# A float32 layer from split products: two more classical chunks, another order of the first product, and a shorter way into the MLP

## The chip, the cores and the metric

The kernel runs on one core of a Trainium2 chip. The metric is the device time of one execution in microseconds (us): the median of several runs. The trace of one profiled execution gives start and length of every instruction on the engines: TensorE (PE, with its weight loads as PEld), VectorE (DVE), ScalarE (ACT), GpSimd (POOL) and SyncE (SP, which issues the DMAs).

## The reference

One layer on 256 tokens of width 1024, all in float32: a mixer with four head groups, and behind it the channel sub-layer on which the change works.

```python
for l in range(DEPTH):                       # DEPTH = 1
    h = rms_norm(x, pre_mix_g[l])
    u = h @ w_in[l]                          # 1024 x 2560
    ...                                      # conformer conv, short conv, attention, RG-LRU
    y = jnp.concatenate([y_a, y_b, y_c, y_d], axis=-1) @ w_out[l]
    x = x + rms_norm(y, post_mix_g[l])
    h = rms_norm(x, pre_mlp_g[l])
    m = jnp.square(jax.nn.relu(h @ mlp_w1[l])) @ mlp_w2[l]   # 1024 x 4096, 4096 x 1024
    x = x + rms_norm(m, post_mlp_g[l])
return x
```

## The kernel before, in words

**Split products.** Every float32 operand is split into a rounded part `hi` and the rest `lo` (ACT copies to `hi`, DVE subtracts to `lo`), and a product is three matmuls: hi·hi, hi·lo and lo·hi. In the trace `hi_w`, `lo_w` are such parts of an MLP weight, `h2T`, `h2L` those of the normalised activations h, and `mh`, `ml` those of m = relu(h W1)².

**Chunks.** The hidden width 4096 is cut into 16 chunks of 256. For chunk c, `up(c)` multiplies h with its columns of W1 into one PSUM bank `pm` (two halves j, eight blocks k, three matmuls each: 48 matmuls of 256 columns). `relu2` reads the bank on ACT (tile `mr`, then the square, tile `mf`). A product with the chunk's rows of W2 follows, accumulated in PSUM banks over the chunks.

**Two forms of the second product.** The product of m and W2 of one chunk is a 2 by 2 by 2 product of blocks. Chunks in `SEVEN` (1 to 12) use a form with seven block products (Strassen's idea, Winograd's sums): `t_sums` forms sums of weight blocks on DVE (tile `trs`), `t_hi`/`t_lo` split them (`th` on ACT, `tl` on DVE), `act_sums` forms sums of m, and `down7` issues 7 x 3 = 21 matmuls of 512 columns. Chunk 0 uses the classical `EIGHT`: 24 matmuls, no sums of weights, and one sum of m. Chunks 13 to 15 go into the final pieces, `last_down(n, t, h)` (chunk n, token tile t, piece h).

**Order.** The instructions of every engine stand in the order in which the program is written. An iteration c of the main loop splits the weights W1 of c+1 and W2 of c, forms and splits the sums, takes relu² of chunk c, issues `down7(c-1)`, and then `up(c+1)`. So PE runs up(c+1), down7(c), up(c+2), down7(c+1) and so on. `up(c+1)` reuses the one bank `pm`, and starts when ACT's `mr` has read chunk c from it. W1 and W2 come as tiles of 1 MiB by DMA into four buffers `raw`.

**Chunk 0** differs: its first product (`pz`, by `up0`) has tokens on the partitions, so `act0`, called between the halves of `up(1)`, transposes m on PE (bank `ptm`), copies it back to `mf`, and forms the sum and the two parts.

**Squares of x.** The last norm needs a factor per token, `q2`, from the sum of squares of `x1`. It is computed ahead of chunk 1: two ACT instructions (tile `scr`) and four short ones on DVE.

Of the kernel before, what the change touches and what calls it, by code (L numbers as in the profile page):

```python
# [16 lines left out]
F32 = mybir.dt.float32  # L17
F32R = mybir.dt.float32r
BF16 = mybir.dt.bfloat16
AF = mybir.ActivationFunctionType  # L20
ALU = mybir.AluOpType
# [3 lines left out]
P = 128  # L25
S = 256
D = 1024
KT = D // P
NW = 2048
# [36 lines left out]
def hybrid_layer(ctx, tc, x, head, win, wout, w1, w2, gates, rows, out):  # L66
    nc = tc.nc
    V, A, G, T, Q = (InOrder(tc, e) for e in (nc.vector, nc.scalar, nc.gpsimd, nc.tensor, nc.sync))

    cst = ctx.enter_context(tc.tile_pool(name="cst", bufs=1))  # L70
    wts = ctx.enter_context(tc.tile_pool(name="wts", bufs=4))
# [3 lines left out]
    wk = wk_ctx.__enter__()  # L75
# [3 lines left out]
    def pbank(tag, name):  # L79
        return pacc.tile([P, 512], F32, tag=tag, name=name)  # L80
# [5 lines left out]
    def sm(name):  # L86
        return in_turn("sm", name)
# [12 lines left out]
    raw, hi, lo = {}, {}, {}  # L100

    def new_raw(n):
        k = seq[n]
        raw[k] = wts.tile([P, NW], F32, tag="raw", name=f"raw_{k[0]}{k[1]}")
        return raw[k], src[k[0]][k[1]]

    def load(n, parts=1):
        if n < len(seq):
            w, d = new_raw(n)
            for i in range(parts):  # L110
                c = slice(i * NW // parts, (i + 1) * NW // parts)
                Q.dma_start(w[:, c], d[:, c])

    def part(i, parts):
        return slice(i * NW // parts, (i + 1) * NW // parts)
# [26 lines left out]
    c = 0  # L142
    for blocks in HEAD:
        n = HOFF[blocks[-1]] + S
        Q.dma_start(hd[:, c:n], head[:, c:n])
        c = n
# [570 lines left out]
    h2 = big.tile([P, KT, S], F32R, tag="hT", name="h2T")  # L717
    h2L = big.tile([P, KT, S], F32R, tag="hL", name="h2L")
# [124 lines left out]
    wk = ctx.enter_context(tc.tile_pool(name="wk2", bufs=2))  # L843
# [13 lines left out]


    FORMS = 13
    SEVEN = range(1, FORMS)  # L860
    BLOCK = {(0, 0): 0, (1, 1): 1, (1, 0): 2, (0, 1): 3}
    B = 512
    mf, mh, ml, th, tl = {}, {}, {}, {}, {}

    def up(c, between=None):
        pu = pbank("mm0", f"pm{c}")
        H, L = hi["w1", c], lo["w1", c]
        for j in range(2):
            if j and between:
                between()  # L870
            o = pu[:, j * S:(j + 1) * S]
            for k in range(KT):
                ws = slice(k * S + j * P, k * S + (j + 1) * P)
                T.matmul(o, H[:, ws], h2[:, k, :], start=(k == 0), stop=False)
                T.matmul(o, H[:, ws], h2L[:, k, :], start=False, stop=False)
                T.matmul(o, L[:, ws], h2[:, k, :], start=False, stop=(k == KT - 1))
        return pu

    def relu2(c, pu):
        r = wk.tile([P, 512], F32, name="mr", bufs=1)  # L880
        A.activation(r, pu, AF.Relu)
        m = mf[c] = wk.tile([P, 8 * P], F32, name="mf", bufs=2)
        A.activation(m[:, :512], r, AF.Square)

    def mblocks(c, i, n=1):
        return mf[c][:, i * P:(i + n) * P]

    def act_sums(c):

        if c not in SEVEN and c < FORMS:  # L890
            pairs = mf[c][:, :4 * P].rearrange("p (i t n) -> p i t n", t=2, n=P)
            V.tensor_tensor(mblocks(c, 4, 2).rearrange("p (i n) -> p i n", n=P), pairs[:, :, 1], pairs[:, :, 0],
                            op=ALU.subtract)
        elif c < FORMS:
            V.tensor_tensor(mblocks(c, 4), mblocks(c, 0), mblocks(c, 1), op=ALU.subtract)
            V.tensor_tensor(mblocks(c, 5, 2).rearrange("p (i n) -> p i n", n=P),
                            mf[c].rearrange("p (i n) -> p i n", n=P)[:, 0:5:4, :],
                            mblocks(c, 2)[:, None, :].to_broadcast([P, 2, P]), op=ALU.add)
            V.tensor_tensor(mblocks(c, 7), mblocks(c, 3), mblocks(c, 6), op=ALU.subtract)

    def act_cols(c):
        return slice(P, 8 * P) if c in SEVEN else slice(0, (6 if c < FORMS else 4) * P)

    def act_hi(c):
        cs = act_cols(c)
        mh[c] = wk.tile([P, 8 * P], F32R, name="mh", bufs=2)
        A.activation(mh[c][:, cs], mf[c][:, cs], AF.Copy)

    def act_lo(c):
        cs = act_cols(c)  # L910
        ml[c] = wk.tile([P, 8 * P], F32R, name="ml", bufs=2)
        V.tensor_tensor(ml[c][:, cs], mf[c][:, cs], mh[c][:, cs].bitcast(F32), op=ALU.subtract)
# [4 lines left out]
    def t_sums(c):  # L917

        if c in SEVEN:
            r = raw["w2", c]  # L920
# [7 lines left out]
    def t_hi(c):  # L928
        if c in SEVEN:
            th[c] = wk.tile([P, NW], F32R, name="th", bufs=2)  # L930
            A.activation(th[c], tr[c], AF.Copy)

    def t_lo(c):
        if c in SEVEN:
            tl[c] = wk.tile([P, NW], F32R, name="tl", bufs=2)
            V.tensor_tensor(tl[c], tr[c], th[c].bitcast(F32), op=ALU.subtract)

    def w2_hi(c):
        k = "w2", c
        hi[k] = wts.tile([P, NW], F32R, tag="hi", name=f"hi_w2{c}")  # L940
        cs = slice(0, 3 * B if c in SEVEN else NW)
        A.activation(hi[k][:, cs], raw[k][:, cs], AF.Copy)

    def w2_lo(c):
        k = "w2", c
        lo[k] = wts.tile([P, NW], F32R, tag="lo", name=f"lo_w2{c}", bufs=3)
        cs = slice(0, 3 * B if c in SEVEN else NW)
        V.tensor_tensor(lo[k][:, cs], raw[k][:, cs], hi[k][:, cs].bitcast(F32), op=ALU.subtract)

    relu2(0, pz[0])  # L950

    def act0():
        pt = sm("ptm")
        m = mf[0]
        for f in range(2):
            for t in range(2):
                T.transpose(pt[:, f * S + t * P:f * S + (t + 1) * P], m[:, t * S + f * P:t * S + (f + 1) * P], ident)
        A.activation(m[:, :512], pt, AF.Copy)
        act_sums(0)
        act_hi(0)  # L960
        act_lo(0)


    PRODUCTS = (("acc0", 1, 0), ("acc1", 3, 2), ("acc2", 7, 1), ("sm0", 5, 4), ("mm1", 4, 5), ("sm1", 6, 6), ("acc3", 2, 7))
# [2 lines left out]
             ("acc2", 5, 1))  # L967
    M = {}

    def down7(c):  # L970
        for tag, a, b in PRODUCTS if c in SEVEN else EIGHT:
            first = tag not in M
            if first:
                M[tag] = pbank(tag, f"m7_{tag}")
            ah, al = mh[c][:, a * P:(a + 1) * P], ml[c][:, a * P:(a + 1) * P]
            H, L = (hi["w2", c], lo["w2", c]) if b < 4 else (th[c], tl[c])
            w = slice(b % 4 * B, (b % 4 + 1) * B)
            T.matmul(M[tag], ah, H[:, w], start=first, stop=False)
            T.matmul(M[tag], ah, L[:, w], start=False, stop=False)
            T.matmul(M[tag], al, H[:, w], start=False, stop=(c == FORMS - 1))  # L980

    cs_ = [trs[:, 0, t * D:(t + 1) * D] for t in range(2)]
    pieces = {}
# [34 lines left out]
    def last_down(n, t, h):  # L1018
        cols, o = pieces[t, h]
        half_ = min(h, 1)  # L1020
        if t and h and n == FORMS:
            for p_ in ("h", "l"):
                T.matmul(o, last["id"], last[p_][:, (h - 1) * 256:h * 256], start=(h == 2 and p_ == "h"), stop=False,
                         skip_group_check=True)
        down(n, t, half_, slice(cols.start - half_ * 512, cols.stop - half_ * 512), o, (t, h) == (0, 1) and n == FORMS,
             n == 15)


    def w1_at(c):
        return 13 + 2 * c  # L1030

    load(18)
    w2_hi(0)
    w2_lo(0)
    for t in range(2):

        scr = few.tile([P, D], BF16, name="scr", bufs=1)
        ss = few.tile([P, 1], F32, name="ss")
        A.activation(scr, x1[t], AF.Square, accum_out=ss)
        V.tensor_scalar(q2[t], ss, 1.0 / D, RMS_EPS, op0=ALU.mult, op1=ALU.add)  # L1040
        V.reciprocal(q2[t], q2[t])
    pm_ = up(1, act0)
    load(19)
    for c in range(1, 16):

        if c == FORMS + 1:
            quarters()
        if c < 15:
            split_hi(w1_at(c + 1))
        if c > 1:  # L1050
            t_sums(c)
        w2_hi(c)
        if c < 15:
            split_lo(w1_at(c + 1))
        if c == 1:
            t_sums(c)
        w2_lo(c)
        load(w1_at(c) + 5)
        t_hi(c)
        relu2(c, pm_)  # L1060
        act_sums(c)
        t_lo(c)
        act_hi(c)
        act_lo(c)
        if c <= FORMS:
            down7(c - 1)
        elif c == FORMS + 1:
            for t, h in sorted(pieces):
                last_down(FORMS, t, h)
        load(w1_at(c) + 6)  # L1070
        if c < 15:
            pm_ = up(c + 1)

# [33 lines left out]
            V.scalar_tensor_tensor(sss[t][:, 1:2], sss[t][:, 1:2], 1.0 / D, sss[t][:, 0:1], op0=ALU.mult, op1=ALU.add)  # L1107

    scrl = few.tile([P, D], BF16, name="scr", bufs=1)
    for h in range(2):  # L1110
        for n in (14, 15):
            last_down(n, 0, h)
        last_sq(0, h)
        if h == 0:
            last_sum(0, 0)
        last_u(0, h)
# [53 lines left out]
```

## Time and profile before

| | |
|---|---|
| median of 3 runs | 289.65 us (288.9 to 290.02) |
| profiled execution, own time | 288.48 us |
| its span, first to last instruction | 286.8 us |
| mean granted clock of TensorE | 0.989 |
| PE busy | 273.0 us (95%) |
| DVE busy | 252.9 us (88%) |
| ACT busy | 185.3 us (65%) |

The own time lies 1.68 us over the span. PE is busy in nearly all of the span, but a busy PE need not be at its peak: a matmul at half the clock, or one whose end is only modelled, counts as busy too. So the rows below are read by the starts of instructions.

### The profile page before, as it was taken

To read this page: it belongs to the slowest core of one execution; us is meant where nothing else is said; L and a number is where in the kernel's file an instruction comes from. 1 tells how busy PE (TensorE), PEld (TensorE's weight loads), DVE (VectorE), ACT (ScalarE), POOL (GpSimd) and SP (SyncE) were. 2 spreads that over 40 slices of the span, in tenths; PEclk is the share of its full clock that TensorE was granted. 3 is DMA by queue.
4 is the path that set the end of the run, shared out by engine and by line. 5 is a ranking of instruction groups with operands and counts; after the bars stand their busy time and mean duration, and the time that the engine had idled before them with its cause. 6 is when DMAs were issued, how large, how long until landed. Compare 5 with 4: busy or idle time off the path is not lost.

```text
span 286.8 us, 4561 instructions
## 1 busy us (share of the span) xinstructions
PE 273.0 (95%) x1824; PEld 243.8 (85%) x1824; DVE 252.9 (88%) x340; ACT 185.3 (65%) x224; POOL 22.3 (8%) x53
## 2 busy tenths in 40 slices
PE   6899999999999998989999999999999999999991
PEld 4699997999877897778998898898898898899781
DVE  1999999899989994879999999999999999978174
ACT  3995469874548849585775775775775775855222
POOL 4388500000000000000000000000000000000000
PEclk9999999999999999799999999999999999999998
DMA  7998436925304544551663573573473574610003
GB/s 228 387 407 338 162 150 245 399 94 207 146 2 155 210 150 166 209 213 57 235 229 136 223 278 103 209 265 126 198 291 111 187 257 157 237 83 2 0 30 117
DMA packets 9236, 53.03 MB, mean 185 GB/s; under 512 B 1024, under 2 KB 1536, under 8 KB 3712
## 3 DMA queue, kind: packets, MB, share of 16 engines
q1 hardware_dynamic: 9216, 52.75, 49.9%
q8 instruction: 14, 0.23, 0.3%
q14 instruction: 6, 0.05, 0.0%
HBM read 51.70 MB, written 1.05 MB: 184 GB/s over the span
## 4 chain that ended last, share of the span: by engine, by line
PE 56%; DVE 30%; ACT 8%; issue 3%; DMA 2%; SPq 0%; DVEq 0%; ACTq 0%
PE pu L60 19%; PE pm L60 14%; DVE lo_w L60 10%; PE acc L60 7%; DVE trs L60 7%; PE m_acc L60 6%; DVE tl L60 5%; ACT th L60 3%; DVE mf L60 2%; DVE ml L60 2%; DMA hd<-in_head_dram 2%; PE c L60 2%; PE pz L60 2%; ACT hi_w L60 1%; ACT mr L60 1%
## 5 line engine op out<-in xcount | busy, mean ns | idle before, releaser
L60 DVE TENSOR_TENSOR lo_w<-raw_w,hi_w 128x2048 fp32r<-128x2048 f32 (+3 forms) x36 | 66.2, 1870 | 5.9 <-ACT hi_w L60 5.9
L60 PE MATMUL pm<-h2T,hi_w 128*128 128x256 f32 x240 | 67.9, 283 | 1.7 <-ACT mr L60 1.2
L60 PE MATMUL pm<-h2T,lo_w 128*128 128x256 f32 x240 | 66.7, 278 | 0.0
L60 PE MATMUL pm<-h2L,hi_w 128*128 128x256 f32 x240 | 66.7, 278 | 0.0
L60 ACT ACTIVATE hi_w<-raw_w 128x2048 fp32r<-128x2048 f32 (+2 forms) x33 | 54.5, 1694 | 1.3 <-issue 1.3
L60 PEld LDWEIGHTS pm<-h2T,hi_w 128*128 128x128 f32 x240 | 45.2, 188 | 5.8 <-ACT mr L60 5.7
L60 PEld LDWEIGHTS pm<-h2T,lo_w 128*128 128x128 f32 x240 | 45.3, 189 | 0.0
L60 PEld LDWEIGHTS pm<-h2L,hi_w 128*128 128x128 f32 x240 | 45.1, 188 | 0.1
L60 ACT ACTIVATE th<-trs 128x2048 fp32r<-128x2048 f32 x12 | 23.0, 1921 | 21.7 <-DVE trs L60 21.7
L60 PE MATMUL pu<-hT,hi_in 128*128 128x256 f32 x128 | 36.3, 283 | 0.0
L60 PE MATMUL pu<-hT,lo_in 128*128 128x256 f32 x128 | 35.8, 280 | 0.0
L60 PE MATMUL pu<-hL,hi_in 128*128 128x256 f32 x128 | 35.8, 280 | 0.0
L60 ACT ACTIVATE mh<-mf 128x896 fp32r<-128x896 f32 (+2 forms) x16 | 14.2, 889 | 21.6 <-DVE mf L60 21.5
L60 DVE TENSOR_TENSOR tl<-trs,th 128x2048 fp32r<-128x2048 f32 x12 | 27.4, 2284 | 0.0
L60 PE MATMUL m_acc<-hi_w,mh 128*128 128x512 f32 (+1 forms) x60 | 23.6, 394 | 2.0 <-ACT mh L60 2.0
L60 DVE SCALAR_TENSOR_TENSOR cacc<-zpad,prm,cacc 128x256 f32<-128x256 f32 x60 | 25.4, 483 | 0.1
L60 PEld LDWEIGHTS pu<-hL,hi_in 128*128 128x128 f32 x128 | 24.3, 190 | 0.0
L60 PEld LDWEIGHTS pu<-hT,lo_in 128*128 128x128 f32 x128 | 24.2, 189 | 0.0
L60 PEld LDWEIGHTS pu<-hT,hi_in 128*128 128x128 f32 x128 | 24.0, 188 | 0.0
L60 PE MATMUL m_acc<-hi_w,ml 128*128 128x512 f32 (+1 forms) x60 | 23.8, 397 | 0.3 <-DVE ml L60 0.3
L60 PE MATMUL m_acc<-lo_w,mh 128*128 128x512 f32 (+1 forms) x60 | 23.4, 391 | 0.0
L60 DVE TENSOR_TENSOR ml<-mf,mh 128x896 fp32r<-128x896 f32 (+2 forms) x16 | 16.0, 1002 | 6.1 <-ACT mh L60 6.1
(232 smaller groups left out, 542.4 us busy)
## 6 DMA issues: line engine op xcount, KB each, us to landing
raw_w<-in_w_dram SPq DMA_DIRECT2D x32, 1024.0 KB, 5.0
raw_in<-in_win_dram SPq DMA_DIRECT2D x7, 1024.0 KB, 6.3
raw_out<-in_wout_dram SPq DMA_DIRECT2D x4, 1024.0 KB, 4.8
raw_in<-in_win_dram SPq DMA_DIRECT2D x4, 512.0 KB, 7.8
hd<-in_head_dram SPq DMA_DIRECT2D x3, 384.0 KB, 5.6
x<-in_x_dram SPq DMA_DIRECT2D x2, 512.0 KB, 7.6
grow<-in_rows_dram SPq DMA_DIRECT2D x2, 512.0 KB, 7.3
hd<-in_head_dram SPq DMA_DIRECT2D x2, 256.0 KB, 4.8
```

The source lines that it names most:

```text
L60: ins = f(*args, **kwargs)
```

## The change

- Chunks 1 and 7 leave `SEVEN`: they use the classical form with 24 matmuls.
- `up(c)` issues its 48 matmuls pass by pass: in each half eight with `hi_w` and `h2T`, eight with `hi_w` and `h2L`, eight with `lo_w` and `h2T`. Before, the three alternated.
- In `down7` the last two of the seven products (weight blocks 6 and 7) are issued in halves of 256 columns: 12 matmuls in place of 6.
- W2 of chunk 0 is split in two parts, the first of them ahead of `relu2(0)`.
- `act0` makes `mh` and `ml` of chunk 0 from the PSUM bank `ptm` itself, in two pieces (the four blocks, then their two sums), without a copy of all of it in `mf`.
- The squares of x move from ahead of chunk 1 to the end of iteration 7, ahead of `up(8)`.
- At the end, for token tile 0, both pieces of chunk 14 stand ahead of those of chunk 15.

```diff
-    SEVEN = range(1, FORMS)
+    SEVEN = (2, 3, 4, 5, 6, 8, 9, 10, 11, 12)
...
-            for k in range(KT):
-                ws = slice(k * S + j * P, k * S + (j + 1) * P)
-                T.matmul(o, H[:, ws], h2[:, k, :], start=(k == 0), stop=False)
-                T.matmul(o, H[:, ws], h2L[:, k, :], start=False, stop=False)
-                T.matmul(o, L[:, ws], h2[:, k, :], start=False, stop=(k == KT - 1))
+            for i, (w, h) in enumerate(((H, h2), (H, h2L), (L, h2))):
+                for k in range(KT):
+                    ws = slice(k * S + j * P, k * S + (j + 1) * P)
+                    T.matmul(o, w[:, ws], h[:, k, :], start=(i == 0 and k == 0), stop=(i == 2 and k == KT - 1))
...
+    def w2_first(i):
+        cs, k = part(i, 2), ("w2", 0)
+        A.activation(hi[k][:, cs], raw[k][:, cs], AF.Copy)
+        V.tensor_tensor(lo[k][:, cs], raw[k][:, cs], hi[k][:, cs].bitcast(F32), op=ALU.subtract)
+
+    w2_first(0)
     relu2(0, pz[0])
...
-        A.activation(m[:, :512], pt, AF.Copy)
-        act_sums(0)
-        act_hi(0)
-        act_lo(0)
+        A.activation(mh[0][:, :512], pt, AF.Copy)
+        V.tensor_tensor(ml[0][:, :512], pt, mh[0][:, :512].bitcast(F32), op=ALU.subtract)
+
+        pairs = pt.rearrange("p (i t n) -> p i t n", t=2, n=P)
+        A.activation(m[:, :256].rearrange("p (i n) -> p i n", n=P), pairs[:, :, 0], AF.Copy)
+        V.tensor_tensor(m[:, 512:768].rearrange("p (i n) -> p i n", n=P), pairs[:, :, 1],
+                        m[:, :256].rearrange("p (i n) -> p i n", n=P), op=ALU.subtract)
+        A.activation(mh[0][:, 512:768], m[:, 512:768], AF.Copy)
+        V.tensor_tensor(ml[0][:, 512:768], m[:, 512:768], mh[0][:, 512:768].bitcast(F32), op=ALU.subtract)
...
-            w = slice(b % 4 * B, (b % 4 + 1) * B)
-            T.matmul(M[tag], ah, H[:, w], start=first, stop=False)
-            T.matmul(M[tag], ah, L[:, w], start=False, stop=False)
-            T.matmul(M[tag], al, H[:, w], start=False, stop=(c == FORMS - 1))
+            parts = 2 if b in (6, 7) else 1
+            for i in range(parts):
+                o, w = M[tag][:, part_of(i, parts)], slice(b % 4 * B + i * B // parts, b % 4 * B + (i + 1) * B // parts)
+                T.matmul(o, ah, H[:, w], start=first and i == 0, stop=False)
+                T.matmul(o, ah, L[:, w], start=False, stop=False)
+                T.matmul(o, al, H[:, w], start=False, stop=(c == FORMS - 1 and i == parts - 1))
...
     load(18)
-    w2_hi(0)
-    w2_lo(0)
-    for t in range(2):
+    w2_first(1)
...
+        if c == 7:
+            token_factor(0)
+            token_factor(1)
...
+    for n in (14, 15):
+        for h in range(2):
+            last_down(n, 0, h)
     for h in range(2):
-        for n in (14, 15):
-            last_down(n, 0, h)
         last_sq(0, h)
```

The order on ACT behind chunk 0's first product, before. `hi_w_1310` is W2 of chunk 0, `hi_w_1386` W1 of chunk 2, `hi_w_1388` W2 of chunk 1; `scr` are the squares of x, `pm_1324` is the bank of `up(1)`.

```order
L60 ACTIVATE h2T<-ptha,prm 128x128 x3
L60 ACTIVATE mr<-pz 128x512
L60 ACTIVATE mf<-mr 128x512
L60 ACTIVATE hi_w_1310<-raw_w_1067 128x2048
L60 ACTIVATE scr,ss<-x_75 128x1024
L60 ACTIVATE scr,ss<-x_76 128x1024
L60 ACTIVATE mf<-ptm 128x512
L60 ACTIVATE mh<-mf 128x768
L60 ACTIVATE hi_w_1386<-raw_w_1295 128x2048
L60 ACTIVATE hi_w_1388<-raw_w_1308 128x1536
L60 ACTIVATE th<-trs 128x2048
L60 ACTIVATE mr<-pm_1324 128x512
```

The same place of ACT now; `hi_w_1304` is W2 of chunk 0, `hi_w_1380` W1 of chunk 2, `hi_w_1382` W2 of chunk 1, `pm_1316` the bank of `up(1)`.

```order
L60 ACTIVATE h2T<-ptha,prm 128x128 x3
L60 ACTIVATE hi_w_1304<-raw_w_1067 128x1024
L60 ACTIVATE mr<-pz 128x512
L60 ACTIVATE mf<-mr 128x512
L60 ACTIVATE hi_w_1304<-raw_w_1067 128x1024
L60 ACTIVATE mh<-ptm 128x512
L60 ACTIVATE mf<-ptm 128x256
L60 ACTIVATE mh<-mf 128x256
L60 ACTIVATE hi_w_1380<-raw_w_1295 128x2048
L60 ACTIVATE hi_w_1382<-raw_w_1312 128x2048
L60 ACTIVATE mr<-pm_1316 128x512
L60 ACTIVATE mf<-mr 128x512
```

The squares are gone from between `mf` and the reading of `ptm`, half of W2 of chunk 0 stands ahead of `mr<-pz`, and no `th<-trs` stands ahead of `mr<-pm`.

The order on DVE at the same place, before; `lo_w_1156` is the second half of W1 of chunk 1, `lo_w_1312` W2 of chunk 0, `lo_w_1390` W1 of chunk 2, `lo_w_1395` W2 of chunk 1, `q` the token factors.

```order
L60 TENSOR_TENSOR lo_w_1156<-raw_w_1065,hi_w_1153 128x1024
L60 TENSOR_TENSOR lo_w_1312<-raw_w_1067,hi_w_1310 128x2048
L60 TENSOR_SCALAR q_0_1095<-ss 128x1
L60 RECIPROCAL q_0_1095<-q_0_1095 128x1
L60 TENSOR_SCALAR q_1_1096<-ss 128x1
L60 RECIPROCAL q_1_1096<-q_1_1096 128x1
L60 TENSOR_TENSOR mf<-mf 128x256
L60 TENSOR_TENSOR ml<-mf,mh 128x768
L60 TENSOR_TENSOR lo_w_1390<-raw_w_1295,hi_w_1386 128x2048
L60 TENSOR_TENSOR trs<-raw_w_1308 128x1024
L60 TENSOR_TENSOR trs<-raw_w_1308,trs 128x512 x2
L60 TENSOR_TENSOR lo_w_1395<-raw_w_1308,hi_w_1388 128x1536
```

The same place of DVE now; `lo_w_1305` is W2 of chunk 0, `lo_w_1384` W1 of chunk 2, `lo_w_1386` W2 of chunk 1, `raw_w_1388` W2 of chunk 2.

```order
L60 TENSOR_TENSOR lo_w_1156<-raw_w_1065,hi_w_1153 128x1024
L60 TENSOR_TENSOR lo_w_1305<-raw_w_1067,hi_w_1304 128x1024 x2
L60 TENSOR_TENSOR ml<-ptm,mh 128x512
L60 TENSOR_TENSOR mf<-ptm,mf 128x256
L60 TENSOR_TENSOR ml<-mf,mh 128x256
L60 TENSOR_TENSOR lo_w_1384<-raw_w_1295,hi_w_1380 128x2048
L60 TENSOR_TENSOR lo_w_1386<-raw_w_1312,hi_w_1382 128x2048
L60 TENSOR_TENSOR mf<-mf 128x256
L60 TENSOR_TENSOR ml<-mf,mh 128x768
L60 TENSOR_TENSOR trs<-raw_w_1388 128x1024
```

The four instructions of `q` are gone from here, `ml` of chunk 0 comes in two pieces, and chunk 1 has no `trs`.

## Rows read from the trace of the kernel before

**Rows 1.** The page's row of engines: busy us, share of the span, instructions.

```profile
PE 273.0 (95%) x1824; PEld 243.8 (85%) x1824; DVE 252.9 (88%) x340; ACT 185.3 (65%) x224; POOL 22.3 (8%) x53
```

**Rows 2.** Stretches: us; PE, PEld, DVE, ACT, POOL busy; granted clock; DMA share, GB/s.

```profile
113.20:123.91 10.71, 7.84 (x27) 5.53 (x25) 8.04 (x9) 6.55 (x7) 0.00 (x0) 0.84 0.54 196
123.91:251.06 127.15, 126.70 (x828) 113.00 (x829) 124.93 (x119) 86.54 (x75) 0.00 (x0) 1.00 0.54 195
251.06:286.80 35.74, 29.10 (x191) 25.82 (x189) 20.18 (x29) 13.82 (x22) 0.00 (x0) 0.96 0.12 44
```

**Rows 3.** Timeline of PE, chunk 0 to 1: start, length, instruction, [idle before, releaser].

```profile
110.01 0.60 PE L60 MATMUL ptm<-ident,mf 128*128 128x128 f32 x4
...
113.09 0.28 PE L60 MATMUL pm<-h2T,lo_w 128*128 128x256 f32 x1
114.76 0.50 PE L60 MATMUL m_acc<-hi_w,mh 128*128 128x512 f32 x1 [1.39 <-ACT mh L60]
...
118.13 0.63 PE L60 MATMUL m_acc<-hi_w,mh 128*128 128x512 f32 x1
118.56 0.63 PE L60 MATMUL m_acc<-lo_w,mh 128*128 128x512 f32 x1
...
122.30 0.40 PE L60 MATMUL m_acc<-hi_w,ml 128*128 128x512 f32 x1
123.91 0.39 PE L60 MATMUL pm<-h2T,hi_w 128*128 128x256 f32 x1 [1.22 <-ACT mr L60]
```

**Rows 4.** Timelines of ACT, then of DVE, in the same stretch.

```profile
107.52 0.60 ACT L60 ACTIVATE mr<-pz 128x512 f32<-128x512 f32 x1 [1.12 <-issue]
...
108.70 1.90 ACT L60 ACTIVATE hi_w<-raw_w 128x2048 fp32r<-128x2048 f32 x1
110.50 1.04 ACT L60 ACTIVATE scr<-x 128x1024 bf16<-128x1024 f32 x1
...
121.46 1.91 ACT L60 ACTIVATE th<-trs 128x2048 fp32r<-128x2048 f32 x1 [3.57 <-DVE trs L60]
123.28 0.58 ACT L60 ACTIVATE mr<-pm 128x512 f32<-128x512 f32 x1
...
106.71 1.22 DVE L60 TENSOR_TENSOR lo_w<-raw_w,hi_w 128x1024 fp32r<-128x1024 f32 x1
110.63 2.29 DVE L60 TENSOR_TENSOR lo_w<-raw_w,hi_w 128x2048 fp32r<-128x2048 f32 x1 [2.71 <-ACT hi_w L60]
```

**Rows 5.** Timeline of DVE over one chunk, the third.

```profile
128.75 1.22 DVE L60 TENSOR_TENSOR trs<-raw_w 128x1024 f32<-128x1024 f32 x1
...
131.34 3.95 DVE L60 TENSOR_TENSOR lo_w<-raw_w,hi_w 128x2048 fp32r<-128x2048 f32 x2
...
136.20 2.29 DVE L60 TENSOR_TENSOR tl<-trs,th 128x2048 fp32r<-128x2048 f32 x1
...
139.40 1.22 DVE L60 TENSOR_TENSOR trs<-raw_w 128x1024 f32<-128x1024 f32 x1
```

**Rows 6.** The chain that ended last: start, length, engine, tile, instructions.

```profile
246.40 2.08 PE m_acc L60 x9
...
251.23 5.66 PE pm L60 x48
...
262.96 5.47 PE pm L60 x48
```

**Rows 7.** Waits: who for whom, us in total, times, longest.

```profile
PEld pm L60 <- ACT mr L60: 5.7, 10, 1.7
```

**Rows 8.** Costliest groups, weight loads of the first product: busy us, mean ns.

```profile
L60 PEld LDWEIGHTS pm<-h2T,hi_w 128*128 128x128 f32 x240 | 45.2, 188 | 5.8 <-ACT mr L60 5.7
```

**Rows 9.** Timelines of PE and of DVE near the end.

```profile
270.44 0.51 PE L60 MATMUL m_acc<-hi_w,mh 128*128 128x512 f32 x1 [0.62 <-ACT mh L60]
...
274.05 0.74 DVE L60 SCALAR_TENSOR_TENSOR u<-trs,q,grow 128x512 f32<-128x512 f32 x1
275.18 0.69 DVE L60 TENSOR_TENSOR trs<-c,trs 128x512 f32<-128x512 f32 x1 [0.39 <-PE c L60]
```

More of the change, by code (lines that the diff above doesn't have):

```diff
@@ L948, in w2_lo @@
         V.tensor_tensor(lo[k][:, cs], raw[k][:, cs], hi[k][:, cs].bitcast(F32), op=ALU.subtract)
+    hi["w2", 0] = wts.tile([P, NW], F32R, tag="hi", name="hi_w20")
+    lo["w2", 0] = wts.tile([P, NW], F32R, tag="lo", name="lo_w20", bufs=3)
+    def w2_first(i):
[3 more added lines that the diff above has]
+    w2_first(0)
     relu2(0, pz[0])
@@ L957, in act0 @@
                 T.transpose(pt[:, f * S + t * P:f * S + (t + 1) * P], m[:, t * S + f * P:t * S + (f + 1) * P], ident)
-        A.activation(m[:, :512], pt, AF.Copy)
-        act_sums(0)
-        act_hi(0)
-        act_lo(0)
+        mh[0] = wk.tile([P, 8 * P], F32R, name="mh", bufs=2)
+        ml[0] = wk.tile([P, 8 * P], F32R, name="ml", bufs=2)
+        A.activation(mh[0][:, :512], pt, AF.Copy)
[6 more added lines that the diff above has]
+        V.tensor_tensor(ml[0][:, 512:768], m[:, 512:768], mh[0][:, 512:768].bitcast(F32), op=ALU.subtract)
     PRODUCTS = (("acc0", 1, 0), ("acc1", 3, 2), ("acc2", 7, 1), ("sm0", 5, 4), ("mm1", 4, 5), ("sm1", 6, 6), ("acc3", 2, 7))
@@ L968, in hybrid_layer, with part_of @@
     M = {}
+    def part_of(i, parts):
+        return slice(i * B // parts, (i + 1) * B // parts)
     def down7(c):
@@ L1032, in hybrid_layer, with token_factor @@
     load(18)
-    w2_hi(0)
-    w2_lo(0)
-    for t in range(2):
+    w2_first(1)
+    def token_factor(t):
         scr = few.tile([P, D], BF16, name="scr", bufs=1)
```

## The prediction

> **What bounds the kernel now.** The page's row of engines comes first: PE is busy for 95% of the span and DVE for 88% [rows 1]. Two engines near their limit mean that the question is which one waits for the other, stage by stage. The span up to the MLP's chunk 0 is not touched by the change, so I cut the rest at three starts of matmuls: 113.20, the end of up(1); 123.91, the start of up(2); 251.06, the start of up(14) [rows 2].
>
> In the first stretch of 10.71 us PE issues one second product (chunk 0, 24 matmuls). The reader should see three losses [rows 3]. PE stops after 113.09 until 114.76, because `mh` of chunk 0 comes late. Then the granted clock falls: at 118.13 matmuls of 512 columns follow each other every 0.43 us, where others take 0.23 (2.08 us for nine, [rows 6]); the mean clock of the stretch is 0.84 [rows 2], so (1 - 0.84) x 10.71 = 1.7 us of full-speed work is lost. Last, after 122.30 up(2) waits until 123.91 for `mr` of chunk 1.
>
> The second stretch, 127.15 us, holds twelve up and twelve down products. DVE is busy for 124.93 us of it, the clock is 1.00 [rows 2]. DVE starts the sums of one chunk at 128.75 and those of the next at 139.40, so it needs 10.65 us for a chunk, without a pause [rows 5]. PE needs less: a down product takes 251.23 - 246.40 = 4.83 us, an up product 5.47 or 5.66 (both lengths occur, [rows 6]), together 10.30 to 10.49. The difference shows as ten waits of the next up product for `mr`, 5.7 us in all [rows 7]; `mr` stands on ACT behind `th`, and `th` waits for DVE's `trs` [rows 4]. So DVE sets the pace here, by a narrow margin, and PE is next.
>
> The last stretch hangs on PE until about 270 and on DVE and ACT behind that [rows 9].
>
> **Chunk 0 and 1.** I follow the new order with the durations of the rows. ACT was idle for 1.12 us ahead of `mr<-pz` at 107.52 [rows 4]. The first half of W2's `hi` now lies there: half of 1.90, about 1.0 us, so `mr` is not late. If that cover were missing, it would cost up to 1.0 us on this chain, which has the slack found next. The square ends at about 108.7, the second half of `hi` at 109.7. The transposes begin at 110.01 and are over at 110.6 [rows 3]. Before, ACT was then still busy with 1.90 of `hi` and twice 1.04 of squares [rows 4], which made `mh` late. Now `mh` of the four blocks is read from PSUM at 110.7 and is there at 111.3 (0.60, as the PSUM read of `mr`). DVE has finished both halves of W2's `lo` by 110.9 (1.22 each; the second waits for ACT's 109.7), makes `ml` by 112.0 (an estimate of 0.65, somewhat over a quarter of the 2.29 for 2048 columns), the sum by 112.4, and ACT and DVE its two parts by 112.8 and 113.2. PE wants `mh` at 113.20, `ml` 0.46 later, and the sum's parts only 18 matmuls on. So nothing is late, with 1.7 us to spare on `ml`. Neither the pause nor the fall of the clock has a cause left, and chunk 0's product takes 24 x 0.231 = 5.55 us: 113.20 to 118.75.
>
> up(2) then needs `mr` of chunk 1. ACT goes on at 112.8 with two `hi` tiles (1.85 apart, to 116.5) and `mr` (117.1). No `th` stands in between, since chunk 1 is classical. DVE has `lo` of W1 of chunk 2 by 116.9 (2.29 behind ACT's 114.6). up(2) starts at 118.75 instead of 123.91: **-5.16 us**.
>
> **The steady stretch.** Each classical chunk takes `trs` (131.34 - 128.75 = 2.59) and `tl` (2.29) from DVE [rows 5], some 0.4 in smaller sums, and gives back a quarter more of W2's `lo` (0.5): about 4.8 us. On ACT `th`, 1.91, goes, and 0.4 of `hi` comes. On PE it adds three matmuls, 24 x 0.231 - 4.83 = 0.7 us. Does this free PE from DVE for good? DVE ends W2's `lo` of chunk 1 at 119.1 and, with the sum (0.4), ACT's `mh` (0.8) and `ml` (0.9) behind it, `ml` of chunk 1 at 121.3; 10.65 later, at 132.0, it ends that of chunk 2. PE runs up(2) and down(1) to 129.9, up(3) to 135.4, and wants chunk 2 then: 3.4 us of slack. It shrinks by 0.16 to 0.35 for each chunk, to 2.0 or more at chunk 6. Chunk 7 gives 4.8 us back and takes in the squares: 2 x 1.04 plus the short reads on ACT, for which DVE's four short instructions wait some 1.6 us behind `ml` of chunk 7, and with them `trs` of chunk 8. That is hidden by the slack, then about 5 us; without it, it would cost 1.6. From there 3 us shrink again until chunk 12. So PE is never late, and the stretch is PE's own work: 12 up + 10 down of 4.83 + 2 of 5.54.
>
> The length of an up product is open. Pass by pass changes no operand shape and no count, only which of three matmuls comes next; no row shows this order. The bounds are the two lengths seen, 5.47 and 5.66 [rows 6]: 65.6 + 59.4 = 125.0, or 67.9 + 59.4 = 127.3, against 127.15. I take eight short and four long, since the waiting starts mostly give the short one: 66.4 + 59.4 = 125.8, **-1.4 us** (-2.2 to +0.1). That `lo_w` is wanted 1.8 us later in each half gains nothing, because `lo_w` is no longer late.
>
> **Halves.** In ten chunks six matmuls of 512 columns become twelve of 256. 6 x 0.231 = 1.39; 12 x 5.47/48 = 1.37; 12 x 5.66/48 = 1.42. So -0.2 to +0.3 us over all; I take **0**.
>
> **The end.** PE waits at 270.44 for `mh` of chunk 15 [rows 9], after six matmuls of chunk 14. With twelve of chunk 14 ahead (2.8 us) that wait is covered. But DVE does the sums in a row: the first piece is finished 0.23 us later (three pieces of 1.39 end later than two and the wait), so `u` of it moves from 274.05 to 274.28 and ends at about 274.95; the sum of the second piece, at 275.18 before, follows there. Behind it the chain is DVE's and ACT's. **-0.2 us** (0 to -0.8, if it all counted). up(14), long before, may be short: **-0.1**.
>
> **Sum.** -5.16 - 1.4 - 0.2 - 0.1 = -6.9 us: 281.6 of own time against 288.48. The profiled execution lies 1.17 under the median of the runs, so the median should be 289.65 - 6.9 = 282.8.
>
> **A rule against it.** Weight loads of 188 ns [rows 8] stand before every matmul, and the halves add 6 x 10 = 60 of them. In the rows 48 pairs of load and matmul take 5.47 us, 0.114 a pair [rows 6], less than one load alone: loads run beside the matmul ahead. The Trainium skill, page "TensorE: Matmul & The Clock Gate", section "The mechanism", says that a weight load overlaps with running matmuls only where they use different row groups of the array; all of these use the whole array. By its figure for a load, 128/1.2 = 107 ns (section "LDWEIGHTS"), 60 exposed loads would be 6.4 us, and the change would come out at about -0.5. The trace does not agree with that rule.
>
> **The rivals.** First, exposed loads as a mechanism of this kernel: if the 60 added loads stood in line with the matmuls at the row's 188 ns, they would cost 11.3 us, and -6.9 would become +4.4: 294, slower. It decides from 0.115 us a load on. Against it: 0.114 us for a load and a matmul together [rows 6]. Loads that hide in part, at 0.09 to 0.14 each, would end within 0.5% of before. The page's rule is of this kind.
>
> Second, a pause of PE stays at chunk 0. My timetable gives `ml` 1.7 us of slack, but it has five handovers between three engines. If PE still stops by 1.5 us and the clock falls again, that is 1.5 + 1.7 us given up: 286. For it speaks that the pause before was 1.55 us and enough; against it, that the squares and half of `hi` are gone from the chain.
>
> Third, the change doesn't free PE, because DVE stays ahead of it by nothing: chunk 2's `trs` begins late, or the squares at chunk 7 cut the slack through. Then the second stretch stays near 127 + 0.6 and only the first term is left: about 285. The slack of 2 us speaks against it.
>
> **How the numbers follow.** My forecast 0.80; pause at chunk 0 0.08; DVE still the bound 0.06; exposed loads 0.06, two thirds of it in full (slower), the rest in part (no change). The likeliest gives 282.8. Its own bounds are -8.3 (all short, the whole end, halves at best) and -5.0 (all long, halves at worst): 281.4 to 284.7. To hold 8 in 10 with the second and third rival on one side, and some tenths of scatter of the median, I take 280.9 to 286.0. Faster by over 0.5% (1.4 us, what a measurement of this kernel can tell from no change): 0.93; within it 0.03; slower 0.04.
>
> **What would show it.** Right: PE without a pause between up(1) and chunk 0's product, clock near 1.00 there, up(2) 10.7 - 5.2 = 5.5 us behind the end of up(1); no waits of `pm` for `mr`; chunks 10.3 to 10.5 us apart and 0.7 more for two of them; DVE with pauses. Wrong: a clock below 1 behind 113, up products longer than 5.66, or `m_acc` waiting for `ml`.

## The result, and the profile after

The median goes from 289.27 to 281.22 us (4 runs each; 287.7 to 290.02 before, 280.92 to 281.82 after): estimated ratio 0.9731, 95% interval 0.9686 to 0.9777 (the quotient of the two medians is 0.972). The profiled execution takes 280.92 us, with a span of 279.2 against 286.8 before: -7.6 us.

The page of the changed kernel, busy time by engine and then the share of the span on the chain that ended last, by engine, answers to [rows 1]:

```profile
PE 270.7 (97%) x1890; PEld 248.3 (89%) x1890; DVE 243.9 (87%) x330; ACT 182.7 (65%) x224; POOL 21.7 (8%) x53
...
PE 93%; DVE 3%; DMA 1%; ACT 1%; issue 1%; DVEq 0%; ACTq 0%
```

The same chain in the kernel before:

```profile
PE 56%; DVE 30%; ACT 8%; issue 3%; DMA 2%; SPq 0%; DVEq 0%; ACTq 0%
```

PE's busy share hardly tells the difference (95% and 97%). The chain does: PE now holds 93% of it instead of 56%, and DVE 3% instead of 30%.

The same three stretches as in [rows 2], cut at the same matmuls (end of up(1), start of up(2), start of up(14), end):

```profile
112.73:118.32 5.59, 5.59 (x26) 4.51 (x25) 4.10 (x3) 4.79 (x5) 0.00 (x0) 1.00 0.40 148
118.32:244.04 125.72, 125.72 (x896) 117.02 (x895) 119.09 (x115) 86.55 (x77) 0.00 (x0) 1.00 0.55 209
244.04:279.20 35.16, 28.35 (x192) 25.77 (x190) 19.74 (x29) 13.83 (x22) 0.00 (x0) 0.96 0.09 31
```

The 7.6 us come apart like this: 113.20 - 112.73 = 0.5 up to the end of up(1); 10.71 - 5.59 = 5.1 at chunk 0; 127.15 - 125.72 = 1.4 in the steady stretch; 35.74 - 35.16 = 0.6 behind it. In the first stretch the clock is 1.00 instead of 0.84, and PE's busy time equals the stretch.

Rows of the timelines of PE, ACT and DVE in the changed kernel (start, length, instruction, idle before and releaser), against [rows 3, 4, 9]:

```profile
112.73 0.39 PE L60 MATMUL m_acc<-hi_w,mh 128*128 128x512 f32 x1
118.09 0.39 PE L60 MATMUL m_acc<-hi_w,ml 128*128 128x512 f32 x1
118.32 1.07 PE L60 MATMUL pm<-h2T,hi_w 128*128 128x256 f32 x8
...
106.88 0.60 ACT L60 ACTIVATE mr<-pz 128x512 f32<-128x512 f32 x1 [0.17 <-issue]
110.10 0.60 ACT L60 ACTIVATE mh<-ptm 128x512 fp32r<-128x512 f32 x1 [1.00 <-PE ptm L60]
116.32 0.57 ACT L60 ACTIVATE mr<-pm 128x512 f32<-128x512 f32 x1
...
110.78 0.69 DVE L60 TENSOR_TENSOR ml<-ptm,mh 128x512 fp32r<-128x512 f32 x1 [0.43 <-ACT mh L60]
130.90 1.08 DVE L60 TENSOR_TENSOR ml<-mf,mh 128x896 fp32r<-128x896 f32 x1
...
173.49 1.08 DVE L60 TENSOR_TENSOR ml<-mf,mh 128x896 fp32r<-128x896 f32 x1
182.45 0.15 DVE L60 TENSOR_SCALAR q<-ss 128x1 f32<-128x1 f32 x1 [0.83 <-ACT scr L60]
267.69 0.68 DVE L60 TENSOR_TENSOR trs<-c,trs 128x512 f32<-128x512 f32 x1
```

The three PE rows have no idle before them. `mh` of chunk 0 is there at 110.7, 2 us before PE wants it. `mr` of chunk 1 has read its bank by 116.89 (116.32 + 0.57), 1.4 us before PE comes to up(2) at 118.32.

### The profile page after: what moved, and what is told of

Same layout as the page of the kernel before. It is cut to its first block, busy times and chain, and to the rows that moved or that the text cites. A ratio compares the mean times of both kernels' runs of the same rounds, so it can differ in the third digit from the quotient of the medians.

```text
span 279.2 us, 4676 instructions
## 1 busy us (share of the span) xinstructions
PE 270.7 (97%) x1890; PEld 248.3 (89%) x1890; DVE 243.9 (87%) x330; ACT 182.7 (65%) x224; POOL 21.7 (8%) x53
## 4 chain that ended last, share of the span: by engine, by line
PE 93%; DVE 3%; DMA 1%; ACT 1%; issue 1%; DVEq 0%; ACTq 0%
PE pm L60 30%; PE pu L60 21%; PE m_acc L60 17%; PE acc L60 7%; PE m_sm L60 7%; PE m_mm L60 2%; PE pz L60 2%; DVE u L60 1%; PE c L60 1%; PE psc L60 1%; DMA hd<-in_head_dram 1%; PE po L60 1%; DVE trs L60 1%; ACT scr L60 1%; PE pg L60 1%
## 5 line engine op out<-in xcount | busy, mean ns | idle before, releaser
L60 PE MATMUL pm<-h2T,hi_w 128*128 128x256 f32 x240 | 32.4, 277 | 0.0
L60 PE MATMUL pm<-h2T,lo_w 128*128 128x256 f32 x240 | 32.2, 276 | 0.0
L60 PE MATMUL pm<-h2L,hi_w 128*128 128x256 f32 x240 | 32.2, 276 | 0.0
L60 PEld LDWEIGHTS pm<-h2T,hi_w 128*128 128x128 f32 x240 | 30.0, 188 | 0.3
L60 PEld LDWEIGHTS pm<-h2T,lo_w 128*128 128x128 f32 x240 | 29.5, 188 | 0.0
L60 PEld LDWEIGHTS pm<-h2L,hi_w 128*128 128x128 f32 x240 | 29.5, 188 | 0.0
L60 ACT ACTIVATE mh<-mf 128x896 fp32r<-128x896 f32 (+3 forms) x16 | 13.6, 848 | 22.2 <-DVE mf L60 22.1
L60 ACT ACTIVATE th<-trs 128x2048 fp32r<-128x2048 f32 x10 | 19.2, 1919 | 13.5 <-DVE trs L60 13.5
L60 DVE TENSOR_TENSOR tl<-trs,th 128x2048 fp32r<-128x2048 f32 x10 | 22.8, 2283 | 0.0
L60 DVE TENSOR_TENSOR ml<-mf,mh 128x896 fp32r<-128x896 f32 (+3 forms) x16 | 15.2, 952 | 7.5 <-ACT mh L60 7.5
```

What stands on the lines that cost most here:

```text
L60: ins = f(*args, **kwargs)
```

## The experiments

Each kernel ran beside the kernel before, on the same chip; ratios are to that. The changed kernel itself was not run again beside them. Its ratio is 0.9731 (0.9686 to 0.9777), and only the intervals of experiments 4 and 5 lie clear of it. So what the other experiments change is read from lengths in the profiles, one profile for each kernel, and their medians do not decide it.

**1. The halves taken back.**

```diff
-            parts = 2 if b in (6, 7) else 1
+            parts = 1
```

> The changed kernel with the last two products of down7 whole again (six matmuls of 512 columns). Theory: the halves are not what makes all up products short; up products stay at 5.45 us, a down product of seven goes from 4.92 to 4.84, so about 0.7 us less in all (280.5). Rival: the halves keep the up products short; then several of the ten up products behind such a down product take 5.66, and the time goes up by as much as 0.2 us each, to 281.5 to 282.5.

Measured: 282.07 us, ratio 0.9773 (0.9748 to 0.9799). The rival holds, by the lengths of the up products. The chain of the changed kernel (start, length, engine, tile, instructions), from up(2) through chunk 2:

```profile
118.48 5.45 PE pm L60 x48
...
129.51 5.45 PE pm L60 x48
134.96 2.09 PE m_acc L60 x9
137.04 0.70 PE m_sm L60 x3
137.74 0.69 PE m_mm L60 x3
138.43 0.72 PE m_sm L60 x6
139.15 0.72 PE m_acc L60 x6
139.87 5.45 PE pm L60 x48
```

The chain with whole products, over the same chunks:

```profile
118.84 5.45 PE pm L60 x48
...
129.86 5.45 PE pm L60 x48
135.31 2.09 PE m_acc L60 x9
...
139.49 0.69 PE m_acc L60 x3
140.18 5.66 PE pm L60 x48
```

Without halves the down product of chunk 2 is shorter (140.18 - 135.31 = 4.87 against 139.87 - 134.96 = 4.91; the later ones take 4.84 against 4.92), but the up product behind it takes 5.66. That is so behind all nine down products of seven that have an up product within the stretch, and behind the tenth, while up products behind a classical chunk stay at 5.45. PE waits for nothing in either kernel. So here the length of an up product depends on what stands ahead of it, and the halves, at 0.05 to 0.08 us a chunk, buy 0.21. The stretch from up(2) to up(14) is 126.89 us without them, 125.72 with them.

**2. The order pass by pass taken back.**

```diff
-            for i, (w, h) in enumerate(((H, h2), (H, h2L), (L, h2))):
-                for k in range(KT):
+            for k in range(KT):
...
+                T.matmul(o, H[:, ws], h2[:, k, :], start=(k == 0), stop=False)
+                T.matmul(o, H[:, ws], h2L[:, k, :], start=False, stop=False)
+                T.matmul(o, L[:, ws], h2[:, k, :], start=False, stop=(k == KT - 1))
```

> The changed kernel with the three kinds of matmul of up(c) alternating again. Theory: the order pass by pass makes up products short; now some or all of the twelve take 5.66 instead of 5.45, 0.8 to 2.5 us more (282 to 283.7). Rival: the order does nothing and only which instruction stands ahead decides; all stay at 5.45, time unchanged.

Measured: 281.08 us, ratio 0.9756 (0.9731 to 0.9782), and a span of 279.2, that of the changed kernel. The rival holds. In its chain:

```profile
139.12 0.72 PE m_acc L60 x6
139.84 5.45 PE pm L60 x48
```

All twelve up products are short with the three kinds alternating. The order pass by pass is worth nothing here. With whole products it makes no difference either: experiment 5 has the old order, experiment 1 the new one, and both take 126.89 us from up(2) to up(14).

**3. Only the last product in halves.**

```diff
-            parts = 2 if b in (6, 7) else 1
+            parts = 2 if b == 7 else 1
```

> The changed kernel with only the last of the seven products in halves (weight block 7), block 6 whole. Theory: what stands right ahead of an up product sets its pitch; six matmuls of 256 columns are enough, up products stay at 5.45, a down product takes 4.88 in place of 4.92: 0.2 to 0.4 us faster than the changed kernel. Rival: the number of whole products ahead sets it; up products go to 5.66 and the time to about 282.5.

Measured: 280.78 us, ratio 0.9727 (0.9696 to 0.9759). In its chain:

```profile
139.67 0.71 PE m_acc L60 x6
140.38 5.44 PE pm L60 x48
```

The theory holds: six matmuls of 256 columns right ahead are enough. No run has halves elsewhere in the product, so that they must stand last is not shown. The stretch from up(2) to up(14) is 125.26 us against 125.72. The medians can't tell the two kernels apart; the lengths in the profile can.

**4. Chunks 1 and 7 with seven products again.**

```diff
-    SEVEN = (2, 3, 4, 5, 6, 8, 9, 10, 11, 12)
+    SEVEN = range(1, FORMS)
```

> The changed kernel with chunks 1 and 7 in the form of seven products again. Theory: DVE is the bound again at 10.65 us a chunk; up(2) waits for mr of chunk 1 behind th, up(14) starts about 5 us later, 285.5 to 287. Rival: the way into the MLP gave the gain and the classical chunks only cost PE 0.7 us each; then it is 1.4 us faster, about 280.

Measured: 286.75 us, ratio 0.9941 (0.9917 to 0.9964). The theory holds. Its chain ahead of up(2), then its waits of PE:

```profile
118.94 0.70 DVE trs L60
119.64 0.02 issue
119.67 1.91 ACT th L60
121.58 0.49 ACT mr L60
122.07 0.04 issue
122.11 5.92 PE pm L60 x48
```

```profile
PEld pm L60 <- ACT mr L60: 5.7, 6, 4.0
```

With chunk 0 done in time, up(2) waits for `trs`, `th` and `mr` of chunk 1, until 122.11 instead of 118.32; later chunks run at DVE's 10.65 us again. Of the 7 to 8 us that the whole change gives, 1.5 are left.

**5. The kernel before with classical chunks 1 and 7, nothing else.**

```diff
-    SEVEN = range(1, FORMS)
+    SEVEN = (2, 3, 4, 5, 6, 8, 9, 10, 11, 12)
```

> The kernel before with chunks 1 and 7 classical, nothing else. Theory: the pause and the fall of the clock at chunk 0 stay, up(2) comes 1.4 us earlier because no th stands ahead of mr; from there PE is the bound, with whole products that leave nine up products at 5.66, about as long as DVE's pace before: 1.5 to 3 us faster than before, 285.3 to 286.8. Rival: the classical chunks alone carry the gain of 7 us; then about 282.

Measured: 286.06 us, ratio 0.9914 (0.9881 to 0.9947), 2.5 us faster than before. The theory holds. Its stretches, from the end of up(1) to up(2) and from there to up(14):

```profile
113.06:122.28 9.22, 7.64 (x26) 5.71 (x25) 6.55 (x7) 6.67 (x8) 0.00 (x0) 0.81 0.58 208
122.28:249.17 126.89, 126.89 (x835) 115.83 (x834) 117.51 (x109) 83.86 (x72) 0.00 (x0) 1.00 0.55 201
```

The pause and the fall of the clock stay (0.81), and PE is busy throughout the second stretch; with whole products that takes 126.89.

**6 to 8. Which part of chunk 0's new way counts.** The squares of x ahead of chunk 1 again:

```diff
+    token_factor(0)
+    token_factor(1)
     pm_ = up(1, act0)
...
-        if c == 7:
-            token_factor(0)
-            token_factor(1)
```

> The changed kernel with the squares of x ahead of chunk 1 again. Theory: mh from PSUM is enough by itself; the squares end at 111.2 instead of nothing, mh of chunk 0 comes at 111.8 and ml at 112.5, PE wants them at 112.7 and 113.2, so no pause, clock 1.00, and the time is the same within 0.3 us. Rival: the squares are what made PE pause; then a pause of about 1.5 us and the fall of the clock return, 2 to 3 us more (283 to 284).

m of chunk 0 through `mf` again:

```diff
-        A.activation(mh[0][:, :512], pt, AF.Copy)
...
+        A.activation(m[:, :512], pt, AF.Copy)
+        act_sums(0)
+        act_hi(0)
+        act_lo(0)
```

> The changed kernel with chunk 0's m copied from PSUM to mf first, as before (squares still at chunk 7). Theory: either of the two, squares moved or m straight from PSUM, is enough; mf at 110.7, the sum at 111.1, mh at 112.0, ml at 112.9, PE wants them at 112.7 and 113.2: no pause, time the same within 0.3 us. Rival: the way through mf is what made PE pause; 2 to 3 us more (283 to 284).

Both edits together:

> Both together: squares ahead of chunk 1 again, and m of chunk 0 through mf. Theory: now mh comes at 113.1 and ml at 114.0, PE pauses some 0.9 us at chunk 0; 282 if the granted clock holds, 283.5 to 284 if it falls. Rival: W2 of chunk 0 in two parts alone has removed the pause; time as the changed kernel's.

Measured: 281.10 us, ratio 0.9751 (0.9729 to 0.9772), for the squares; 281.86, ratio 0.9752 (0.9709 to 0.9795), through `mf`; 282.48, ratio 0.9797 (0.9766 to 0.9829), with both. In the first two PE starts chunk 0's product without a wait; in the second it waits once for `ml`, 0.3 us by the weight loads. With both its timeline shows:

```profile
113.44 0.50 PE L60 MATMUL m_acc<-hi_w,mh 128*128 128x512 f32 x1 [0.53 <-ACT mh L60]
...
114.43 0.50 PE L60 MATMUL m_acc<-hi_w,ml 128*128 128x512 f32 x1 [0.27 <-DVE ml L60]
```

So either edit alone is enough, and each hides what the other is worth. With both taken back PE waits half as long as before (0.53 + 0.27 against 1.39 + 0.27 us), and the clock stays up (1.00 from 112.5 to 125). That the rest is due to W2 of chunk 0 in two parts is read from ACT's timeline: `mf<-ptm` starts 4.3 us behind `mr<-pz` there, 5.2 before, because half of `hi` lies ahead of `mr<-pz`. No run takes this edit back by itself.

**9. The old order at the end.**

```diff
-    for n in (14, 15):
-        for h in range(2):
+    for h in range(2):
+        for n in (14, 15):
             last_down(n, 0, h)
-    for h in range(2):
         last_sq(0, h)
```

> The changed kernel with the old order of the last products of token tile 0 (chunks 14 and 15 of one piece, then of the other). Theory: PE waits again about 0.6 us for mh of chunk 15, but behind it DVE's and ACT's chain sets the end: from the end of up(15) to the end of the span 18.5 us in place of 18.2, 0.2 to 0.4 us more. Rival: PE's wait counts in full, 0.8 us or more.

Measured: 281.65 us, ratio 0.9763 (0.9727 to 0.9798). Its timeline has the old wait:

```profile
263.38 0.51 PE L60 MATMUL m_acc<-hi_w,mh 128*128 128x512 f32 x1 [0.62 <-ACT mh L60]
```

From the start of the product behind up(15), 261.21, to the end of the span, 279.7, it takes 18.5 us, against 279.2 - 261.01 = 18.2 in the changed kernel. The theory holds: 0.3 us, and not the 0.8 at which PE's wait would count in full.

**10. One classical chunk, squares in the gap of chunk 15.** With the last product alone in halves:

```diff
-    SEVEN = (2, 3, 4, 5, 6, 8, 9, 10, 11, 12)
+    SEVEN = range(2, FORMS)
...
+        if c == 15:
+            token_factor(0)
+            token_factor(1)
         relu2(c, pm_)
...
-        if c == 7:
-            token_factor(0)
-            token_factor(1)
```

> The changed kernel with chunk 7 in the form of seven products again, only the last product in halves, and the squares of x ahead of relu2 of chunk 15, where ACT and DVE are idle. Theory: DVE's lead of 2.9 us at chunk 2 shrinks by 0.33 a chunk and is used up just at the end; PE saves 0.7 (three matmuls) and 0.4 (halves), and may wait 0.5 at chunks 11 and 12: 0.5 to 1.1 us faster than the changed kernel, about 280.4. Rival: chunk 7 is needed, DVE is late well before chunk 12 and waits start at chunk 8; 1 us or more slower than the changed kernel.

Measured: 280.91 us, ratio 0.9738 (0.9711 to 0.9764). Its stretch from up(2) to up(14), and its chain ahead of up(13):

```profile
117.59:242.87 125.28, 125.23 (x866) 115.14 (x865) 122.85 (x117) 85.84 (x74) 0.00 (x0) 1.00 0.55 206
```

```profile
227.11 1.15 DVE trs L60
...
229.79 1.92 ACT th L60
231.71 0.49 ACT mr L60
232.24 5.92 PE pm L60 x48
```

125.28 is the length of experiment 3. The three matmuls saved at chunk 7 come back as waits at the last two up products of the stretch, where DVE's lead is used up, and as a long up product behind such a wait (its matmuls are 0.118 us apart; the 5.92 of the chain count from the release of the first weight load). So a second classical chunk costs 0.7 us and saves as much. From the end of up(1) to the end of the span this variant and that of experiment 3 both take 166.0 us, the changed kernel 166.5. Neither theory nor rival came true: what is gained is that of the halves alone, and by the medians none of the three is faster.

## Why the prediction was right

**Chunk 0 and 1, -5.16 forecast, -5.12 measured.** The timetable held step for step: `mr<-pz` was not late, `mh` of chunk 0 took 0.60 from PSUM, `mr` of chunk 1 came before up(2) could start. The 24 matmuls took 5.59 (5.55 forecast), and `ml` had the 1.7 us to spare that were forecast. What the timetable did not say is that the edits are redundant (experiments 6 to 8). "Neither the pause nor the fall of the clock has a cause left" came true.

**DVE's lead.** Forecast 3.4 us at chunk 2 and 2.0 or more at chunk 6. At chunk 2 `ml` ends at about 131.9, and PE starts that product at 134.79: 2.9. At chunk 6 `ml` ends at about 174.5, and PE starts that product at 176.26: 1.8. So the lead was smaller than forecast, and still enough. The squares hold DVE at chunk 7 as said: `trs` of chunk 8 starts at 182.72, 1.5 us behind the end of `ml` (1.6 forecast). No wait of `pm` for `mr` is left. That both parts of the change are needed for this shows in experiments 4 and 5: 1.5 and 2.5 us alone, 7 to 8 together. Each removes one of two bounds that lay close behind one another.

**The steady stretch, -1.4 forecast, -1.43 measured, by two errors that cancel.** I took four long up products of twelve; none is long, 12 x 5.45 = 65.4, 1.0 us less than my 66.4. I took nothing for the halves, with +0.3 as the upper bound; a down product is 4.92 instead of 4.83, since matmuls of 256 columns follow each other every 0.120 us there (0.72 for six), and not every 0.114 to 0.118 as in up products: ten chunks, +0.9, and +0.1 for the two classical ones (5.58 instead of 5.54). That the sum came out is luck. The step that failed is the reason for the up products' length: "the waiting starts mostly give the short one". Eight short and four long is what the kernel before has from up(2) to up(13), where ten of the twelve start behind a wait; in the changed kernel none does. Experiments 1 and 3 show that there the product ahead sets the length, experiment 2 that the order within the up product does not. The halves, which I costed at zero as an edit of their own, are what makes the up products short.

**The end, -0.2 forecast.** Experiment 9 gives -0.3 in the profile, by the mechanism named: the sum of the second piece follows `u` of the first, at 267.69 without a wait. up(14) went from 5.66 to 5.45, -0.2 instead of -0.1.

**Exposed weight loads.** The halves add six pairs of load and matmul to a down product and 0.09 us: 15 ns a pair, far from the 188 ns of a load or from the 115 ns that would decide. The trace does not bear out the rule that the Trainium skill, page "TensorE: Matmul & The Clock Gate", section "The mechanism", gives for loads on the same rows of the array.

**What the sum did not have** is the 0.5 us up to the end of up(1): 0.65 us ahead of up(1), which no edit touches and which are read below, less 0.18 that up(1) itself took longer. From the end of up(1) on, the span is 7.1 us shorter, against my 6.9. The profiled execution took 280.92 us, and I had forecast 281.6. The median missed by more, 281.22 against 282.8. I carried over that the median lies 1.17 us above the profiled execution; it now lies 0.30 above. So 281.22 lies at the low end of the range, and just outside the bounds of the sum itself, 281.4 to 284.7. What brought it there is this difference and the 0.5 us, not the mechanism. The kernel before had medians of 288.25 to 289.27 us in the result and beside the experiments, so the 8.05 us between the two medians are uncertain by about one.

## What to carry to other kernels

Where two engines run at 10.3 and 10.65 us a step, relieve the slower one only as far as its lead needs: an algorithm that saves work on one engine at the cost of the other can be left out for a few steps, here two chunks of twelve. Relieving one bound alone gave 1.5 or 2.5 us, both together 7 to 8, so an edit that shows little by itself may be waiting for its partner. And follow the work between engines by a timetable of starts; busy shares said 95% and 97%.

## What was not expected of the hardware

**Two pitches of the same matmuls.** Streams of the same 256-column matmuls go at one of two paces, 5.45 or 5.66 us for 48 (0.114 or 0.118 us each), at a granted clock of 1.00, and a stream mostly keeps its pace to its end. Where an up product starts on time, what stands ahead decides in these runs: whole products of seven gave the long one in all ten cases of experiment 1 and in all ten of experiment 5, halves the short one in all ten of the changed kernel, classical products the short one. One case of the kernel before fits badly. There up(4) takes the short pace behind a whole product of seven, 150.29 - 144.84 = 5.45 us from its first matmul to that of the next product. Its first matmul is not late, but `mr` ends only 0.05 us ahead of its first weight load:

```profile
144.84 0.28 PE L60 MATMUL pm<-h2T,hi_w 128*128 128x256 f32 x1
...
150.29 0.39 PE L60 MATMUL m_acc<-hi_w,mh 128*128 128x512 f32 x1
```

Where an up product starts late, even by 0.1 us, either pace comes up, with halves ahead too. In experiment 4 ten of them start late, and four take the long pace, three of these behind halves. In one of the three, eight matmuls take 156.42 - 155.47 = 0.95 us, 0.118 each:

```profile
155.47 1.11 PE L60 MATMUL pm<-h2T,lo_w 128*128 128x256 f32 x8
156.42 1.11 PE L60 MATMUL pm<-h2T,hi_w 128*128 128x256 f32 x8
```

Why is open; no run here takes the weight loads apart from the matmuls.

At one place either pace comes up, with nothing changed ahead of it. The chain of the changed kernel and, below it, that of the kernel before, at the first 200 matmuls of the input projection:

```profile
13.33 23.50 PE pu L60 x200
```

```profile
13.13 24.34 PE pu L60 x200
```

0.84 us, and no edit lies ahead of it. It is 23.5 in six of the twelve profiles and 24.3 in the other six, four of them of variants of the changed kernel, so it is not the change's. Each kernel has one profile, so whether it differs from kernel to kernel or from execution to execution is not shown. A comparison of two profiles should take it out first.

**A pause does not always lower the clock.** Before, PE stood still from 113.20 to 114.76, 1.56 us, soon after it once more for 0.27, and the clock fell to half behind that (matmuls of 512 columns every 0.43 us instead of 0.23, the lower of the two levels, 1.2 GHz). In experiment 4 PE waits 3.6 us ahead of up(2), and the granted clock of that stretch stays 1.00:

```profile
112.77:122.11 9.34, 5.74 (x26) 4.33 (x24) 6.91 (x6) 5.73 (x6) 0.00 (x0) 1.00 0.54 199
```

In experiment 8 pauses of 0.53 and 0.27 us left it at 1.00 too. So whether a pause brings a fall, and with it the 1.7 us that it cost before, can't be told from its length alone. What made the clock fall there stays open.
